# A transformer layer's input projection in an order written by hand, with its filling work dealt anew

## The chip, the core and the metric

The kernel runs on one core of one Trainium2 chip. The metric is device time of one execution in microseconds (us), lower is better. A core has five engines that run side by side, each with its own queue of instructions in a fixed order: TensorE (PE, matrix products), VectorE (DVE), ScalarE (ACT), GpSimd (POOL) and SyncE (SP, which here only issues DMA transfers). Products land in PSUM, which DVE and ACT read; everything else lives in SBUF.

## The reference, cut to what matters

One decoder layer on 1024 tokens of width 1024, in float32:

```
xn   = rmsnorm(h, pre_mix_norm)
proj = xn @ w_in                       # queries, keys, gates of retention, latents cq, ckv, kr
ret  = silu(rg) * groupnorm(retention(rope(rq), rope(rk), rv))
mla  = softmax(causal(q @ k^T)) @ v    # 8 heads; q, k, v from rmsnorm(cq), rmsnorm(ckv), rope(kr)
mix  = concat([ret, mla]) @ w_o
h    = h + rmsnorm(mix, post_mix_norm)
hn   = rmsnorm(h, pre_ffn_norm)
h    = h + rmsnorm((silu(hn @ w_gate) * (hn @ w_up)) @ w_down, post_ffn_norm)
h    = h + rmsnorm(p @ w_ple_proj, ple_norm) * sigmoid(h @ w_ple_gate + b)
```

## The kernel before, in words

Every matrix product is made of three: each operand is split into a high part (an ACT cast, L81) and the rest (a DVE subtraction, L82), and high x high, low x high and high x low are summed in PSUM. The sequence is cut into 8 row tiles of 128 tokens.

**Input projection of the latents** (`pa`, to 82 us). For each tile: x is loaded (`xt`), ACT squares it with a row sum (L186), DVE and POOL make the factor (`rsqrt`: L111 on DVE, a power on POOL L113), DVE multiplies (L188, with the norm weights `wpre`, which a DMA has copied to all partitions), PE turns eight blocks of 128x128 (`ptf`, L175), ACT and DVE split the result into `bh` and `bl`, and PE does 48 products of 336 columns (`pa`, L94). The weights come in six transfers `raw_a`, each split into `hi_a` and `lo_a`. ACT and DVE then norm the result (L241 to L250). The rotary tables (some 20 small DVE instructions from L258 on and two Sin on ACT, after the load of the positions `posi`) are written behind the loop. A scheduler in the build chooses each engine's order from the program and its own cost figures, so work of different tiles and tables lies mixed.

**Attention** (375 to 563 us). Eight heads, two column groups each; a group ends with `os` (L648) and its store to `mo`. Between the groups PE gets pieces of filling work: for the first heads preparations, and from head 2 on pieces of the output projection's retention part (`fill` into `od`, 16 pieces of 12 products with 512 columns), dealt by the line `advance(gen, "fo"[gg], ...)` in the head loop.

**Output projection and norms** (563 to 680 us, `project(n)` and `operands(n)`). For each tile n, `mo` is loaded, split (`mh` by ACT, `ml` by POOL; two buffers each), PE does 24 products `po` into a PSUM tile pair (two buffers), DVE adds `od` (L715), ACT squares with a row sum (L717; the squares themselves are of no use and go to the PSUM tile), then factor, scale and add (L719, L720), a second Square (L723, again into the PSUM tile), scale (L725, L726). `operands(n)` turns the result with PE (`ptx`); for tiles 4 to 7 POOL first makes sums and differences of tile pairs (L739 to L742). After it come the first gate and up products (`gu`), whose weights are loaded to `graw` and `duo[0]` and summed by POOL (`weight_sums`, L793 to L796). From 680 us to about 1080 us `gu` runs, then the down projection, then the last gate.

Of the kernel before, what the change touches and what calls it, by code (L numbers as in the profile page):

```python
# [62 lines left out]
def hybrid_layer(ctx: ExitStack, tc: tile.TileContext, a: dict, out: bass.AP):  # L63
# [105 lines left out]
    def to_features(src, t, tags, bh, bl):  # L169
        ts = slice(t * P, (t + 1) * P)  # L170
        for c in range(2):
            pt = ps1("ptf", tags[c])
            for i in range(4):
                k = 4 * c + i
                pe.transpose(pt[:, i * P : (i + 1) * P], src[:, k * P : (k + 1) * P], ident)  # L175
            v = pt.rearrange("p (k n) -> p k n", k=4)
            split(bh[c][:, :, ts], bl[c][:, :, ts], v)

# [5 lines left out]
    def norm_in(t, xt):  # L184
        ss = small.tile([P, 1], F32, name="ss")
        act.activation(cq[:, t, :512].bitcast(BF16), xt, AF.Square, accum_out=ss)  # L186
        rsqrt(ss, ss, 1.0 / D)
        dve.scalar_tensor_tensor(out=xt, in0=xt, scalar=ss, in1=wpre, op0=ALU.mult, op1=ALU.mult)  # L188
        to_features(xt, t, "tt", bh, bl)
# [7 lines left out]
    for i in range(0, 16, AB):
        m = min(AB, 16 - i)
        stage = tabs.tile([P, S], F32, tag=["tcos", "tsin"][i // AB - 4], name=f"raw_a{i}") if i // AB >= 4 else None
        wa.append(slot(a["w_a"][i : i + m].rearrange("b p n -> p b n"), AC * m, name=f"a{i}", stage=stage))  # L200
        if i // AB == 3:
            xt = load_in(1)
# [4 lines left out]


# [15 lines left out]
    for t in range(NT):  # L224
        if t:
            norm_in(t, xt)
            if t + 1 < NT:
                xt = load_in(t + 1)
        pt = ps2(f"pa{t}")
        ca, cb = pt[:, 0:AC], pt[:, 512 : 512 + AC]  # L230
        for c, dst in ((0, ca), (1, cb)):
            products(
                dst,
                [
                    (*bx(k, slice(t * P, (t + 1) * P)), wa_of(0, k, c), wa_of(1, k, c))
                    for k in range(8)
                ],
            )
        sst = small.tile([P, 3], F32, name="sst")
        dst = cq[:, t, :]  # L240
        act.activation(dst[:, :AC], ca, AF.Square, scale=_f32(QL**-0.5), accum_out=sst[:, 0:1])  # L241
        act.activation(dst[:, AC:QL], cb[:, : QL - AC], AF.Square, scale=_f32(QL**-0.5), accum_out=sst[:, 2:3])
        act.activation(dst[:, QL : QL + KVL], cb[:, QL - AC : QL - AC + KVL], AF.Square, scale=_f32(KVL**-0.5),
                       accum_out=sst[:, 1:2])
        dve.tensor_tensor(out=sst[:, 0:1], in0=sst[:, 0:1], in1=sst[:, 2:3], op=ALU.add)
        fac = small.tile([P, 2], F32, name="fac")
        rsqrt(fac, sst[:, 0:2], 1.0)
        dve.tensor_scalar(out=dst[:, :AC], in0=ca, scalar1=fac[:, 0:1], scalar2=None, op0=ALU.mult)
        dve.tensor_scalar(out=dst[:, AC:QL], in0=cb[:, : QL - AC], scalar1=fac[:, 0:1], scalar2=None, op0=ALU.mult)
        dve.tensor_scalar(out=dst[:, QL : QL + KVL], in0=cb[:, QL - AC : QL - AC + KVL], scalar1=fac[:, 1:2],  # L250
                          scalar2=None, op0=ALU.mult)
        act.copy(out=krt[:, t, :], in_=cb[:, QL - AC + KVL : AC])

    RA, HR = RD // 2, ROPE // 2
    posi = tb.tile([P, NT], I32, name="posi")
    sp.dma_start(out=posi, in_=a["pos"])
    posf = tb.tile([P, NT], F32, name="posf")
    dve.tensor_copy(out=posf, in_=posi)  # L258
    angm, sin, cos = [tb.tile([P, NT, HR], F32, name=n) for n in ("angm", "msin", "mcos")]
    dve.tensor_tensor(  # L260
        out=angm,
        in0=posf.unsqueeze(2).broadcast_to([P, NT, HR]),
        in1=inv.unsqueeze(1).broadcast_to([P, NT, HR]),
        op=ALU.mult,
    )
    rotary(angm, sin, cos)
# [2 lines left out]
    dve.tensor_copy(out=mc[:, :, :HR], in_=cos)
    dve.tensor_copy(out=mc[:, :, HR:], in_=cos)  # L270
    dve.tensor_scalar(out=ms[:, :, :HR], in0=sin, scalar1=-1.0, scalar2=None, op0=ALU.mult)
    dve.tensor_copy(out=ms[:, :, HR:], in_=sin)
# [432 lines left out]
    def project(n):  # L705
# [462 lines left out]
```

## Time and profile before

| | |
|---|---|
| median of 3 runs | 1399.54 us (1396.53 to 1400.5) |
| profiled execution | 1400.68 us |
| its span in the trace | 1398.9 us, so 1.8 us lie outside |
| PE busy | 1336.5 us, 96% of the span |
| DVE, ACT, POOL busy | 770.9, 541.8, 461.8 us |

Times in rows are from the span's start. A row of the timeline names its start, its duration, the engine, the line, the operation, the tile written and read, how many alike follow, and in brackets the idle time of that engine ahead of it and what ended it.

### The profile page before, as it was taken

What the parts mean: (1) busy time and instruction counts of PE and PEld (TensorE: products, weight loads), DVE (VectorE), ACT (ScalarE), POOL (GpSimd) and SP (SyncE); (2) the same over time, 40 slices, a digit from 0 to 9 for tenths busy, and PEclk for the clock granted to TensorE, in tenths of its full rate; (3) what the DMA queues carried; (4) which work ended last, traced back from release to release, by engine and by line L of the source; (5) the groups of instructions that cost most, each with busy time, mean ns of one, the idle gap of its engine ahead of it and who ended that gap; (6) DMA issues with size and microseconds to landing.
All of it is one profiled execution on the core that took longest, in us unless ns stands there. A gap on an engine that the chain in (4) does not pass through costs nothing.

```text
span 1398.9 us, 18091 instructions
## 1 busy us (share of the span) xinstructions
PE 1336.5 (96%) x6756; PEld 1134.4 (81%) x6756; DVE 770.9 (55%) x1193; ACT 541.8 (39%) x898; POOL 461.8 (33%) x341
## 2 busy tenths in 40 slices
PE   7999999999989999887999999999999999999997
PEld 6987988988778887665788888888888788888886
DVE  6445637445566676488445444444445554474645
ACT  5443321011565555355343333333334444344521
POOL 1100000000363333248577666666664100012500
PEclk9999999999999999998999999999999999999999
DMA  7127831212474641743344344433346876565422
GB/s 251 46 92 250 265 118 39 75 23 60 143 232 123 200 131 30 273 135 123 121 165 149 146 173 173 169 138 144 140 178 218 269 234 211 178 218 193 138 102 75
DMA packets 85304, 214.73 MB, mean 153 GB/s; under 512 B 8992, under 2 KB 23840, under 8 KB 79584
## 3 DMA queue, kind: packets, MB, share of 16 engines
q1 hardware_dynamic: 85216, 213.58, 45.5%
q8 instruction: 53, 0.87, 0.3%
q14 instruction: 35, 0.29, 0.1%
HBM read 144.86 MB, written 67.63 MB: 152 GB/s over the span
## 4 chain that ended last, share of the span: by engine, by line
PE 83%; DMA 4%; DVE 4%; POOL 3%; issue 3%; ACT 2%; SPq 1%; DVEq 0%; ACTq 0%; POOLq 0%
PE gu L834 29%; PE db L1011 7%; PE pqk L94 6%; PE pg L94 6%; PE da L1011 6%; PE pa L94 4%; PE fill L94 3%; PE prv L94 3%; PE sc L94 3%; PE ptp L630 2%; PE prg L94 2%; PE pge L94 2%; PE po L642 1%; PE pq L94 1%; PE po L641 1%
## 5 line engine op out<-in xcount | busy, mean ns | idle before, releaser
L834 PE MATMUL gu<-x,gh 128*128 128x512 f32 x1232 | 383.6, 393 | 6.3 <-ACT po L723 5.6
L834 PEld LDWEIGHTS gu<-x,gh 128*128 128x128 f32 x1232 | 233.2, 190 | 55.7 <-ACT po L723 5.8
L834 PE MATMUL gu<-x,gl 128*128 128x512 f32 x616 | 241.2, 392 | 0.4 <-DVE gl L82 0.4
L834 PEld LDWEIGHTS gu<-x,gl 128*128 128x128 f32 x616 | 116.7, 189 | 25.1 <-DVE gl L82 0.7
L845 ACT COPY duo<-gu 128x512 f32<-128x512 f32 x66 | 38.9, 589 | 189.3 <-PE gu L834 189.3
L621 POOL TENSOR_TENSOR pr<-pr,ri 128x128 f32<-128x128 f32 (+3 forms) x64 | 74.8, 1178 | 105.7 <-DVE ri L620 98.4
L113 POOL TENSOR_TENSOR s<-s,mhalf 128x1 f32<-128x1 f32 x32 | 23.9, 752 | 238.4 <-DVE s L111 238.3
L113 POOL TENSOR_TENSOR gf<-gf,mhalf 128x4 f32<-128x4 f32 x8 | 8.1, 1008 | 266.7 <-DVE gf L111 266.7
L82 DVE TENSOR_TENSOR gl<-strip,gh 128x1024 fp32r<-128x1024 f32 (+1 forms) x44 | 61.6, 1399 | 33.3 <-ACT gh L81 33.3
L82 DVE TENSOR_TENSOR x<-draw,x 128x1024 fp32r<-128x1024 f32 (+1 forms) x43 | 48.1, 1135 | 46.9 <-ACT x L81 46.9
L82 DVE TENSOR_TENSOR gl<-graw,gh 128x1024 fp32r<-128x1024 f32 x22 | 33.8, 1538 | 72.5 <-ACT gh L81 72.5
L81 ACT CAST x<-draw 128x1024 fp32r<-128x1024 f32 (+1 forms) x47 | 45.2, 979 | 73.0 <-PE db L1011 20.6
L82 DVE TENSOR_TENSOR gl<-duo,gh 128x1024 fp32r<-128x1024 f32 x22 | 29.5, 1343 | 67.9 <-ACT gh L81 67.9
L850 DVE TENSOR_TENSOR duo<-gu,duo 128x512 f32<-128x512 f32 x66 | 45.4, 687 | 38.0 <-PE gu L834 37.9
L82 DVE TENSOR_TENSOR tl<-ptp,th 128x512 fp32r<-128x512 f32 (+1 forms) x80 | 49.8, 633 | 24.7 <-ACT th L81 23.7
L94 PE MATMUL pg<-x,x 128*128 128x512 f32 (+1 forms) x255 | 58.9, 378 | 0.0
L81 ACT CAST th<-ptp 128x512 fp32r<-128x512 f32 (+1 forms) x80 | 42.4, 544 | 41.9 <-PE ptp L630 41.6
L855 POOL TENSOR_TENSOR duo<-duo 128x512 f32<-128x512 f32 x11 | 23.3, 2122 | 103.2 <-DVE duo L818 103.2
L617 ACT ACTIVATE pr<-sc,nm 128x128 f32<-128x128 f32 (+3 forms) x64 | 47.7, 747 | 18.7 <-DVE nm L612 11.1
L94 PEld LDWEIGHTS pg<-x,x 128*128 128x128 f32 x255 | 45.8, 188 | 8.6
L612 DVE CUSTOM_DVE_ANT_0 sc<-sc,cmask 128x128 f32<-128x128 f32 (+3 forms) x64 | 48.0, 770 | 7.7 <-PE sc L94 7.3
L94 PE MATMUL pqk<-bl,hi_r 128*128 128x512 f32 x128 | 50.7, 396 | 0.0
(368 smaller groups left out, 3418.5 us busy)
## 6 DMA issues: line engine op xcount, KB each, us to landing
draw<-ld SPq DMA_DIRECT2D x58, 256.0 KB, 3.8
graw<-in_w_gate SPq DMA_DIRECT2D x11, 1024.0 KB, 8.6
duo<-in_w_up SPq DMA_DIRECT2D x11, 1024.0 KB, 4.7
duo<-in_w_down SPq DMA_DIRECT2D x11, 1024.0 KB, 5.1
td<-duo SPq DMA_DIRECT2D x11, 1024.0 KB, 4.4
ld<-duo SPq DMA_DIRECT2D x11, 1024.0 KB, 4.4
draw<-td SPq DMA_DIRECT2D x36, 256.0 KB, 4.1
ld<-duo SPq DMA_DIRECT2D x11, 768.0 KB, 6.7
```

The costliest lines, as they stand in the source:

```text
L81: act.copy(out=hi, in_=src)
L82: sub.tensor_tensor(out=lo, in0=src, in1=hi.bitcast(F32), op=ALU.subtract)
L94: pe.matmul(dst, l, r, start=(m == 0), stop=(m == n - 1))
L113: pool.tensor_tensor(out=dst, in0=dst, in1=mhalf[:, :n], op=ALU.pow)
L612: dve.tensor_tensor_reduce(out=sv, in0=sv, in1=cmask[:, S - n :].rearrange("p (c n) -> p c n", c=nc_), scale=-1.0, scalar=3.0e38, op0=ALU. ...
L617: act.activation(pr_[:, :n].rearrange("p (c n) -> p c n", c=nc_), sv, AF.Exp, bias=nm, scale=-1.0, accum_out=rs)
L621: pool.tensor_tensor(out=pr_[:, :n], in0=pr_[:, :n], in1=ri.broadcast_to([P, n]), op=ALU.mult)
L630: pe.transpose(pt[:, m * P : (m + 1) * P], pb[qq][:, kk * P : (kk + 1) * P], ident)
L834: pe.matmul(dst, l[:, at, ks], r[:, k, :], start=(n in (0, 1, 3) and x == 0), stop=(x == 11), skip_group_check=True)
L845: act.copy(out=s[nm], in_=dst)
L850: dve.tensor_tensor(out=s[nm], in0=dst, in1=s[nm], op=ALU.add)
L1011: pe.matmul(banks[j], l[:, ls], r[:, rs_], start=(fresh and q == 0 and m == 0), stop=(q == NQ - 1 and m == 2), skip_group_check=True)
```

## The change

Six things are changed.

1. The input projection is written as one function `head()`, whose instructions keep the order in which they stand (`tc.manual_schedule()`). Tiles 0 and 1 are computed side by side, by weight transfer: `part(t, i)` is the nine products of tile t with the weights of transfer i. x of tile 1 is loaded ahead of the weights.
2. The norm weights are loaded as one row of 4 KB, not as a 512 KB copy for all partitions. PE spreads the row with two products against ones (`spread`), and DVE copies the result (L247).
3. PE gets 9 and 12 products on ones without use (`turn`) ahead of and behind the spreading.
4. The rotary tables are one block, after tile 4.
5. `FILL` deals the output projection's pieces otherwise: before, heads 2 to 5 had 3 each, heads 6 and 7 one each, and 2 were left for the end; now heads 2 to 7 have 1, 3, 2, 2, 2 and 3 (the last three inside the last column group of head 7), and 3 are left.
6. The squares of no use in `project` go to a free corner of SBUF (`xt[6]`), so that DVE's add is the PSUM tile's last reader. The first gate weights go to `duo[0]` and the first up weights to the tile `graw`, the other way round than before.

```diff
-    norm_in(0, xt)
...
+    def head():
+        junk = ps1("turn", "f")[:, :P]
+
+        def turn(n):
+            for _ in range(n):
+                pe.matmul(junk, minus, minus, start=True, stop=True)
+
+        sp.dma_start(out=wpre[:1], in_=a["w_pre"])
+        xts = [load_in(0)]
...
+        def half(t, c):
+            pt = ps1("ptf")
+            for i in range(4):
+                k = 4 * c + i
+                pe.transpose(pt[:, i * P : (i + 1) * P], xts[t][:, k * P : (k + 1) * P], ident)
+            ts = slice(t * P, (t + 1) * P)
+            split(bh[c][:, :, ts], bl[c][:, :, ts], pt.rearrange("p (k n) -> p k n", k=4))
+            if c and t + 2 < NT:
+                xts.append(load_in(t + 2))
...
+        pt = ps2("spread")
+        turn(9)
+        for c in range(2):
+            cs = slice(c * 512, (c + 1) * 512)
+            pe.matmul(pt[:, cs], minus[:1], wpre[:1, cs], start=True, stop=True)
+        dve.tensor_copy(out=wpre, in_=pt)
+        turn(12)
+        ss = [squares(0), squares(1)]
+        norm(0, ss[0])
+        weights()
+        half(0, 0)
...
+        for t in range(2, NT):
+            pas[t] = ps2(f"pa{t}")
+            for k in range(8):
+                in_product(t, k, 0)
+            if t + 1 < NT:
+                ready(t + 1)
+            evict(t - 1)
+            if t + 1 < NT:
+                half(t + 1, 0)
+                half(t + 1, 1)
+            for k in range(8):
+                in_product(t, k, 1)
+            if t == 4:
+                tables()
+        evict(NT - 1)
...
+    FILL = (0, 1), (2, 1), (1, 1), (1, 1), (1, 1), (0, 0)
...
+                    if h == NH - 1 and g == 3 and jj < 3:
+                        advance(gen, "o", 1)
...
-                advance(gen, "fo"[gg], (2, 1)[gg] if h < 6 else 1 - gg)
+                advance(gen, "fo"[gg], FILL[h - 2][gg])
...
+        junk = xt[6][:, :, :, 3 * P :].rearrange("p h k n -> p (h k) n")
         ss = small.tile([P, 1], F32, name="s3")
-        act.activation(pt, mix, AF.Square, accum_out=ss)
+        act.activation(junk, mix.rearrange("p (b n) -> p b n", b=8), AF.Square, accum_out=ss)
...
+    sp.dma_start(out=duo[0].rearrange("p (i n) -> p i n", i=4), in_=a["w_gate"][0])
...
-    graw = [pg_.tile([P, 4, HALF], F32, name="graw"), quad[0]]
+    graw = [quad[0], pg_.tile([P, 4, HALF], F32, name="graw")]
```

What this does to the order of instructions is shown at three places. The first is DVE's queue in the input projection, between the split of tile 5 and the factor of tile 6 (`ss`; `angm`, `mc`, `ms` are the tables). After the change:

```order
L323 TENSOR_SCALAR angm<-angm 128x128
L325 SCALAR_TENSOR_TENSOR angm<-angm 128x128
L326 TENSOR_SCALAR angm<-angm 128x128
L346 COPY mc<-mcos 128x8x16
L347 COPY mc<-mcos 128x8x16
L348 TENSOR_SCALAR ms<-msin 128x8x16
L349 COPY ms<-msin 128x8x16
L111 TENSOR_SCALAR ss<-ss 128x1
L236 SCALAR_TENSOR_TENSOR xt<-xt,ss,wpre 128x1024
```

These are the last seven of 20 table instructions in a row, and tile 6's factor and scaling stand behind them. Before the change the tables lay between the work of tiles 1 to 3:

```order
L217 SCALAR_TENSOR_TENSOR angm<-mcos,angm 128x128
L217 SCALAR_TENSOR_TENSOR angm<-msin,angm 128x128
L111 TENSOR_SCALAR ss<-ss 128x1
L217 SCALAR_TENSOR_TENSOR angm<-mcos,angm 128x128
L248 TENSOR_SCALAR cq<-pa_235,fac 128x336
L249 TENSOR_SCALAR cq<-pa_235,fac 128x48
```

So the tables have moved from early and scattered to late and in one piece.

The second place is ACT's queue at the start of the output projection (`mh` are the splits for the tiles in order, the ACTIVATE rows are the Squares and scalings of the norms). Before:

```order
L81 CAST mh_5759<-strip_5743 128x512
L81 CAST mh_5805<-strip_5743 128x512
L717 ACTIVATE po3_5763,s3_5789<-duo3_5741 128x1024
L81 CAST mh_5851<-duo2_5740 128x512
L723 ACTIVATE po3_5763,s3_5796<-duo4_5742 128x1024
L717 ACTIVATE po3_5809,s3_5835<-duo0_5738 128x1024
```

After the change:

```order
L81 CAST mh_5790<-strip_5774 128x512
L81 CAST mh_5836<-strip_5774 128x512
L81 CAST mh_5882<-duo2_5771 128x512
L81 CAST mh_5941<-duo2_5771 128x512
L81 CAST mh_6000<-strip_5774 128x512
L803 ACTIVATE x6_5765,s3_5820<-duo3_5772 128x8x128
L81 CAST mh_6058<-strip_5774 128x512
L809 ACTIVATE x6_5765,s3_5827<-duo4_5773 128x8x128
```

Tile 0's first Square now stands behind five splits, where it stood behind two.

The third place is POOL's queue ahead of the first operand sums (L739 before and L825 after are the first sum of tile 4; L793 and L880 the first of a weight block; L113 the power of a norm's factor). After:

```order
L113 TENSOR_TENSOR s_6030<-s_6030,mhalf 128x1
L880 TENSOR_TENSOR strip<-graw 128x512
L883 TENSOR_TENSOR graw<-graw 128x512
L113 TENSOR_TENSOR s_6037<-s_6037,mhalf 128x1
L113 TENSOR_TENSOR s_6088<-s_6088,mhalf 128x1
L825 TENSOR_TENSOR duo_5772<-duo_5769,duo_5772 128x512
```

Before, all eight weight sums stood between the operand sums of tiles 6 and 7:

```order
L742 TENSOR_TENSOR duo_5740<-duo_5740,duo_5742 128x512
L793 TENSOR_TENSOR strip<-duo_5738 128x512
L113 TENSOR_TENSOR s_6199<-s_6199,mhalf 128x1
L796 TENSOR_TENSOR duo_5738<-duo_5738 128x512
L793 TENSOR_TENSOR strip<-graw 128x512
```

Two of the eight have moved ahead of tile 4's operands; the other six stay where they were.

## Rows read from the trace of the kernel before

**Rows 1.** The page's first part: span, and busy time of PE.

```profile
span 1398.9 us, 18091 instructions
...
PE 1336.5 (96%) x6756; PEld 1134.4 (81%) x6756; DVE 770.9 (55%) x1193; ACT 541.8 (39%) x898; POOL 461.8 (33%) x341
```

**Rows 2.** Windows: length, then busy (count) of each engine, granted clock, DMA share, GB/s.

```profile
426.36:550.00 123.64, 118.36 (x743) 105.48 (x741) 87.22 (x204) 68.65 (x151) 49.62 (x42) 1.00 0.46 132
550.00:562.90 12.90, 10.40 (x46) 8.34 (x46) 4.81 (x9) 6.28 (x12) 1.89 (x1) 0.74 0.05 11
550.00:675.00 125.00, 97.57 (x418) 76.89 (x419) 80.89 (x92) 56.51 (x92) 62.39 (x49) 0.87 0.44 155
```

**Rows 3.** PE's waits: for what, us in total, times, longest.

```profile
PE po L94 <- ACT po L723: 9.2, 6, 3.6
...
PE gu L834 <- ACT po L723: 5.6, 1, 5.6
```

**Rows 4.** Timeline of the input projection, engines mixed.

```profile
9.49 1.21 DVE L82 TENSOR_TENSOR lo_a<-raw_a,hi_a 128x1008 fp32r<-128x1008 f32 x1 [1.73 <-ACT hi_a L81]
...
24.39 0.28 DVE L217 SCALAR_TENSOR_TENSOR angm<-msin,angm 128x128 f32<-128x128 f32 x1
...
32.54 0.42 PE L94 MATMUL pa<-hi_a,bh 128*128 128x336 f32 x1 [1.05 <-ACT bh L81]
...
58.03 0.33 SPq L181 DMA_DIRECT2D xt<-in_x  x1
...
61.66 1.06 ACT L186 ACTIVATE cq<-xt 128x1024 bf16<-128x1024 f32 x1 [0.75 <-DMA xt<-in_x]
...
62.84 0.15 DVE L111 TENSOR_SCALAR ss<-ss 128x1 f32<-128x1 f32 x1 [1.21 <-ACT cq L186]
63.72 1.28 DVE L188 SCALAR_TENSOR_TENSOR xt<-xt,ss,wpre 128x1024 f32<-128x1024 f32 x1 [0.72 <-POOL ss L113]
```

**Rows 5.** Timeline of attention from head 1's last `os` to the filling behind it.

```profile
426.36 0.68 DVE L648 TENSOR_TENSOR os<-po,os 64x512 f32<-64x512 f32 x1
...
548.63 0.95 PE L630 MATMUL ptp<-pack,pr 128*128 128x128 f32 x7
...
554.84 1.72 PE L630 MATMUL ptp<-pack,pr 128*128 128x128 f32 x7
...
562.93 0.69 DVE L648 TENSOR_TENSOR os<-po,os 64x512 f32<-64x512 f32 x1 [1.26 <-ACT os L647]
```

**Rows 6.** Timeline of the output projection's start, ACT, DVE and PE.

```profile
571.91 0.39 PE L94 MATMUL po<-bh,mh 128*128 128x512 f32 x1
572.13 0.39 PE L94 MATMUL po<-bl,mh 128*128 128x512 f32 x1
...
579.32 1.03 ACT L717 ACTIVATE po<-duo 128x1024 f32<-128x1024 f32 x1 [7.80 <-DVE duo L715]
...
581.32 1.28 DVE L719 SCALAR_TENSOR_TENSOR duo<-duo,s,strip 128x1024 f32<-128x1024 f32 x1 [0.67 <-POOL s L113]
```

**Rows 7.** Timeline of POOL's sums, and of PE at the first products of tile 4 to 7.

```profile
623.02 1.29 POOL L739 TENSOR_TENSOR duo<-duo,duo 128x512 f32<-128x512 f32 x1
...
649.46 1.30 POOL L793 TENSOR_TENSOR strip<-duo 128x512 f32<-128x512 f32 x1 [0.64 <-DMA duo<-in_w_up]
...
664.26 1.29 POOL L795 TENSOR_TENSOR strip<-duo,strip 128x512 f32<-128x512 f32 x1
...
670.61 1.27 POOL L742 TENSOR_TENSOR duo<-duo,duo 128x512 f32<-128x512 f32 x1
...
671.25 1.52 PE L834 MATMUL gu<-x,gh 128*128 128x512 f32 x2 [0.68 <-ACT x L81]
...
679.39 1.47 PE L686 MATMUL ptx<-pack,duo 128*128 128x128 f32 x12
```

**Rows 8.** Groups of instructions by line: the Squares into PSUM, and into SBUF.

```profile
L723 ACT ACTIVATE po<-duo 128x1024 f32<-128x1024 f32 x8 | 8.2, 1026 | 14.3 <-DVE duo L720 14.3
...
L186 ACT ACTIVATE cq<-xt 128x1024 bf16<-128x1024 f32 x8 | 8.5, 1058 | 7.5 <-DMA xt<-in_x 7.5
```

More of the change, by code (lines that the diff above doesn't have):

```diff
@@ L123, in hybrid_layer @@
     mhalf = const.tile([P, 32], F32, name="mhalf")
+    minus = const.tile([P, P], F32, name="minus")
+    pool.memset(minus, 1.0)
     pool.memset(mhalf, -0.5)
@@ L168, in hybrid_layer @@
     cq = pa.tile([P, NT, AW], F32, name="cq")
[L169 to L177, printed above, removed]
     def load_in(t):
@@ L182, in load_in @@
         return xt
[L184 to L189, printed above, removed]
     krt = tb.tile([P, NT, ROPE], F32, name="krt")
-    xt = load_in(0)
-    sp.dma_start(out=wpre, in_=a["w_pre"].broadcast_to([P, D]))
-    sp.dma_start(out=pack, in_=a["pack"])
-    norm_in(0, xt)
     wa = []
[L197 to L202, printed above, removed]
     def wa_of(n, k, c):
@@ L206, in wa_of, with in_product, weights, ready @@
         return wa[i // AB][n][:, (i % AB) * AC : (i % AB + 1) * AC]
+    def in_product(t, k, c):
+        xh, xl = bx(k, slice(t * P, (t + 1) * P))
+        wh, wl = wa_of(0, k, c), wa_of(1, k, c)
+        for m, (l, r) in enumerate(((xh, wh), (xh, wl), (xl, wh))):
+            pe.matmul(pas[t][:, c * 512 : c * 512 + AC], l, r, start=(k == 0 and m == 0), stop=(k == 7 and m == 2))
+    def head():
[5 more added lines that the diff above has]
+        xts = [load_in(0)]
+        sp.dma_start(out=pack, in_=a["pack"])
+        xts.append(load_in(1))
+        raw_a = []
+        for i in range(0, 16, AB):
+            m = min(AB, 16 - i)
+            raw = tabs.tile([P, S], F32, tag=["tcos", "tsin"][i // AB - 4], name=f"raw_a{i}") if i // AB >= 4 else (
+                raws.tile([P, S], F32, tag="raw", name=f"raw_a{i}"))
+            raw = raw[:, : AC * m]
+            sp.dma_start(out=raw.rearrange("p (b n) -> p b n", b=m), in_=a["w_a"][i : i + m].rearrange("b p n -> p b n"))
+            raw_a.append(raw)
+        def weights():
+            i = len(wa)
+            wa.append([t[:, : raw_a[i].shape[1]] for t in pair(f"a{i}")])
+            split(*wa[i], raw_a[i])
+        def ready(t):
+            norm(t, squares(t))
+        def half(t, c):
[7 more added lines that the diff above has]
+                xts.append(load_in(t + 2))
+        def squares(t):
+            s = small.tile([P, 1], F32, name="ss")
+            act.activation(cq[:, t, :512].bitcast(BF16), xts[t], AF.Square, accum_out=s)
+            return s
+        def norm(t, s):
+            rsqrt(s, s, 1.0 / D)
+            dve.scalar_tensor_tensor(out=xts[t], in0=xts[t], scalar=s, in1=wpre, op0=ALU.mult, op1=ALU.mult)
+        def part(t, i):
+            for kc in range(i * AB, min(i * AB + AB, 16)):
+                in_product(t, kc // 2, kc % 2)
+        pt = ps2("spread")
[9 more added lines that the diff above has]
+        half(0, 0)
+        for t in range(2):
+            pas[t] = ps2(f"pa{t}")
+        part(0, 0)
+        norm(1, ss[1])
+        weights()
+        half(0, 1)
+        part(0, 1)
+        half(1, 0)
+        part(1, 0)
+        weights()
+        part(0, 2)
+        half(1, 1)
+        part(1, 1)
+        for i in range(3, 6):
+            weights()
+            part(0, i)
+            if i == 3:
+                part(1, 2)
+        ready(2)
+        evict(0)
+        part(1, 3)
+        half(2, 0)
+        half(2, 1)
+        part(1, 4)
+        part(1, 5)
+        for t in range(2, NT):
+            pas[t] = ps2(f"pa{t}")
+            for k in range(8):
[11 more added lines that the diff above has]
+        evict(NT - 1)
@@ new lines, in evict @@
+    def evict(t):
+        pt = pas[t]
+        ca, cb = pt[:, 0:AC], pt[:, 512 : 512 + AC]
+        sst = small.tile([P, 3], F32, name="sst")
+        dst = cq[:, t, :]
+        act.activation(dst[:, :AC], ca, AF.Square, scale=_f32(QL**-0.5), accum_out=sst[:, 0:1])
+        act.activation(dst[:, AC:QL], cb[:, : QL - AC], AF.Square, scale=_f32(QL**-0.5), accum_out=sst[:, 2:3])
+        act.activation(dst[:, QL : QL + KVL], cb[:, QL - AC : QL - AC + KVL], AF.Square, scale=_f32(KVL**-0.5),
+                       accum_out=sst[:, 1:2])
+        dve.tensor_tensor(out=sst[:, 0:1], in0=sst[:, 0:1], in1=sst[:, 2:3], op=ALU.add)
+        fac = small.tile([P, 2], F32, name="fac")
+        rsqrt(fac, sst[:, 0:2], 1.0)
+        dve.tensor_scalar(out=dst[:, :AC], in0=ca, scalar1=fac[:, 0:1], scalar2=None, op0=ALU.mult)
+        dve.tensor_scalar(out=dst[:, AC:QL], in0=cb[:, : QL - AC], scalar1=fac[:, 0:1], scalar2=None, op0=ALU.mult)
+        dve.tensor_scalar(out=dst[:, QL : QL + KVL], in0=cb[:, QL - AC : QL - AC + KVL], scalar1=fac[:, 1:2],
+                          scalar2=None, op0=ALU.mult)
+        act.copy(out=krt[:, t, :], in_=cb[:, QL - AC + KVL : AC])
@@ L209, in rotary @@
+    pas = {}
     def rotary(ang, kh, kl):
@@ L222, in rotary @@
         act.activation(kl, ang, AF.Sin)
[L224 to L252, printed above, removed]
@@ L254, in hybrid_layer @@
-    RA, HR = RD // 2, ROPE // 2
[L255 to L266, printed above, removed]
+    RA, HR = RD // 2, ROPE // 2
@@ L267, in hybrid_layer, with tables @@
     mc = tb.tile([P, NT, ROPE], F32, name="mc")
     ms = tb.tile([P, NT, ROPE], F32, name="ms")
[L269 to L272, printed above, removed]
+    def tables():
+        posi = tb.tile([P, NT], I32, name="posi")
+        sp.dma_start(out=posi, in_=a["pos"])
+        posf = tb.tile([P, NT], F32, name="posf")
+        dve.tensor_copy(out=posf, in_=posi)
+        angm, sin, cos = [tb.tile([P, NT, HR], F32, name=n) for n in ("angm", "msin", "mcos")]
+        dve.tensor_tensor(
+            out=angm,
+            in0=posf.unsqueeze(2).broadcast_to([P, NT, HR]),
+            in1=inv.unsqueeze(1).broadcast_to([P, NT, HR]),
+            op=ALU.mult,
+        )
+        rotary(angm, sin, cos)
+        dve.tensor_copy(out=mc[:, :, :HR], in_=cos)
+        dve.tensor_copy(out=mc[:, :, HR:], in_=cos)
+        dve.tensor_scalar(out=ms[:, :, :HR], in0=sin, scalar1=-1.0, scalar2=None, op0=ALU.mult)
+        dve.tensor_copy(out=ms[:, :, HR:], in_=sin)
@@ L275, in hybrid_layer @@
+    with tc.manual_schedule():
+        head()
     kr = tb.tile([P, NT, ROPE], F32, name="kr")
@@ L887, in when @@
         todo[i].append((f, args))
-    load(0)
     load(1)
```

2 lines of the change are left out of this document (1 added, 1 removed).

## Prediction

> **What bounds the kernel now.** I read the page's busy times first: PE works 1336.5 of 1398.9 us [rows 1], so a gain must come from the 62 us in which it idles, or from stretches at the lower of its two clock levels (1.2 GHz, not 2.4). The windows say where these lie. From 550 to 675 us PE works 97.57 of 125 us, 27.4 idle, at a mean granted clock of 0.87; from head 1's end to 550 it works 118.36 of 123.64, 5.3 idle; in attention's last 12.9 us it is busy 10.40 at 0.74 [rows 2]. Nearly everything else is PE-bound. PE's waits name the releasers: `po` waited 9.2 us and `gu` 5.6 for the Squares that go to PSUM [rows 3]. DVE is busy 80.89 of the 125 us and POOL 62.39 [rows 2], so behind those waits stands a chain of norms that needs ACT, DVE and POOL in turn. Removing a wait on PSUM helps only as far as this chain comes earlier too.
>
> The profiled execution took 1400.68 us, 1.8 outside its span and 1.1 above the median of 1399.54. I sum against 1400.68 and take off 1.1 at the end.
>
> **Input projection, tiles side by side.** Before, the first split of weights runs on DVE at 9.49 and tile 2's first product starts at 32.54, after 1.05 of waiting [rows 4]. Afterwards the first product is still bound by x, the spread weights and `lo_a`. I walk DVE's queue: copy of `spread` (1.2), tile 0's scaling (1.28) to about 9.5, then six `lo_a` of 1.21 (the last a third), and four splits and tile 1's scaling between them [rows 4]. Tile 0's products then need transfer 3's weights at 22, and the last of both tiles end, with tile 2 turned as well, near 31: 1.5 us earlier than 32.54. The 4 KB row instead of 512 KB saves a transfer's place in the queue, but x of tile 1 takes that place. The bounds: 3 earlier if the splits never hold PE, and 3 later if the 23 added products run at the low level, end behind x, and hold tile 0's turning (seven turnings of 128 columns take 1.72 us at the low level and 0.95 at the full one [rows 5]; if a product on ones is worth two of them, the 21 take some 10 us instead of 6, beside the spreading: an estimate). I take -1.5.
>
> The clock here is told by the rows: attention's seven turnings take 0.95 us at 548.63 and 1.72 at 554.84, after PE had stood still several times [rows 5], so an idle PE falls to the lower level. The Trainium skill ("TensorE: Matmul & The Clock Gate", section "What's actually happening") says that the throttled state is the default and activity releases it. By that rule the products on ones would give the first products the full level; whether DVE's splits let PE use it is the walk above.
>
> **Input projection, tables.** Twenty table instructions on DVE, 0.28 or a little less each [rows 4], are some 4.5 us, and hid between other work before. Now they stand in one piece ahead of tile 6's factor, and wait for the positions, whose load is queued behind the last x. Such an x was issued at 58.03 and the Square that waits for it ran at 61.66, 3.6 later [rows 4]. From the middle of tile 4, where the last x is now issued (about 54), the block starts at 55.5 to 58, and with the two Sin and ACT's Square behind them tile 6's factor is 5 to 8 us later; the chain factor, power, scaling takes 62.84 to 65.0 [rows 4]. PE wants the turned tile at about 61, and gets it at 63.4 to 66: it stands 2 to 5 us, since the second half of tile 5 is queued behind those turnings. I take 3.5, between both ends. If tile 5's own work covered it, it would cost nothing. The input projection together: +2.0, from -3 to +8.
>
> **Attention with the pieces dealt anew.** A piece is 12 products 0.22 apart [rows 6], 2.7 us. Heads 2 to 7 had 14, now 13: -2.7. Head 7 now has three at its end. There PE idled 2.5 of 12.9 us [rows 2], and the row of turnings at 1.72 against 0.95 [rows 5] shows about 6 us at half speed, 3 us lost; both can be filled: -5.4. The dealing among heads 2, 4, 5 and 6 is neutral as long as PE paces them, which 118.36 of 123.64 says. So `os` of head 7, at 562.93, comes 8.1 earlier. Bounds: -2.7, if other engines pace the heads with few pieces, and -12, if most of the 5.3 goes too.
>
> **Output projection.** With the Squares off PSUM, PE runs tiles 0 to 5 in one go. But ACT's order puts five `mh` ahead of tile 0's first Square, and the fifth needs a buffer that the third tile's products free. On the basis of the old end of attention: `po` starts at 571.91 [rows 6], 12 `po`, 12 of the left-over piece and 60 `po` take 19.1, `mh` 0.6, the Square with its sum 1.2, the power and waits 0.9, so the first scaling (L719) is at 593.9 instead of 581.32 [rows 6], 12.6 later. Behind it on ACT are every later norm and operand; who waits is DVE, then POOL.
>
> Then the norms catch up, since three adds and most splits are done by then. The next fixed point is POOL's first sum for tile 4, at 623.02 [rows 7]. Two weight sums now stand ahead of it, whose load waits for the last `po`: 156 products from 571.91 reach 607, with the last two tiles and the turnings between them 620, the load some 7, the sums 3.5, so 630.5 to 635.4 with the waits for norms. From 623.02 to the end of tile 7's sums at 671.9 are 48.9; the eight weight sums in it (649.46 to 665.55 [rows 7]) are six now, 4 to 8 us less. Tile 4 to 7's first products, at 671.25 [rows 7], thus come 7.5 to 12.4 later less 4 to 8: -0.5 to +8.3, and I take +5.0 near the upper middle, because the late start of the norms shows in each of these numbers.
>
> The 24 products behind (671.25 to 679.39, 8.1 us) ran partly at the low level; at 0.23 each they take 5.5. If PE no longer stands still just ahead of them, -2.6.
>
> Sixteen Squares now write SBUF. The row with PSUM as target has 1026 ns, the one with SBUF 1058 [rows 8]: 0.03 each, 0.5 us on an engine that is not full. The swap of `graw` and `duo[0]` turns places round and I find no queue that it delays later: 0. The Trainium skill ("ScalarE: Activation LUTs", section "Step-by-step: what each stage is for") says that ACT writes PSUM faster than SBUF, which speaks against this edit; it states no price, and by the two rows the sum stays.
>
> **Sum.** 2.0 - 8.1 + 5.0 - 2.6 = -3.7: 1397.0 against the profiled execution, 1396 against the median.
>
> **Rivals.**
> *The norms catch up wholly* (and the tables are covered): -8.1 - 2.6 = -10.7, 1389. For it: PSUM waits of 14.8 us vanish [rows 3], and DVE has 44 us free in the 125. Against: ACT's order.
> *Slower: the late first norm isn't caught up.* 12.6 late less 8.1, with PE standing ahead of the operands as now, so at the low level again, and 2.0: +6.5, 1406. It decides from a catch-up under some 2 us of the 12.6, or under 5 if the clock is not regained. For it: DVE worked at 65% and POOL at 50% of that stretch [rows 2], each waiting on the other.
> *The pieces don't pace attention*: only -2.7 there, and 1401, no change.
>
> **How the numbers follow.** A measurement tells about 0.3% (4.2 us) from no change, so faster is below 1395.3, slower above 1403.7. Chances: the sum as it stands 0.47, with its own range 1391 to 1402 (0.20 of it faster, 0.25 same, 0.02 slower); full catch-up 0.22, faster; no catch-up 0.19, slower; attention not paced 0.12 (0.08 same, 0.04 slower). Together faster 0.42, same 0.33, slower 0.25. I predict 1396; the range 1385 to 1408 reaches from beyond full catch-up to beyond none.
>
> **What would show it.** Right: attention's last `os` near 555; a gap of 2 to 5 us on PE ahead of tile 6's turning, with DVE on table work; the first scaling 3 to 5 us later than 581.32; POOL's first sum of tile 4 behind two weight sums; the products behind the last operands at the full level. Wrong: the last `os` at 560 or beyond; no gap at tile 6; PE's idle time from 550 to 675 hardly under 27 us, or under 15; a transfer of the gate or up weights that ends the wait ahead of `gu`.

## The result, and the profile after

The changed kernel takes 1413.84 us (median of 4 runs, 1412.82 to 1419.22) against 1399.38 of the kernel before beside it: 1.0119 times, interval 1.0095 to 1.0143. It is slower by 14 us, and outside the predicted range. I read the page first, then windows of the stretches of [rows 2].

```profile
span 1411.7 us, 18196 instructions
...
PE 1346.3 (95%) x6802; PEld 1141.2 (81%) x6802; DVE 770.5 (55%) x1194; ACT 541.7 (38%) x898; POOL 462.2 (33%) x342
```

Windows of after: length, then busy time (count) of PE, PE's loads, DVE, ACT and POOL, granted clock, DMA share, GB/s.

```profile
550.00:675.00 125.00, 96.35 (x453) 77.70 (x452) 80.02 (x98) 55.27 (x92) 54.21 (x44) 0.85 0.44 159
571.00:625.00 54.00, 50.61 (x227) 41.11 (x228) 25.08 (x27) 15.38 (x25) 13.75 (x13) 1.00 0.60 225
625.00:675.00 50.00, 26.29 (x108) 19.82 (x108) 42.66 (x48) 29.09 (x48) 34.80 (x27) 0.62 0.41 139
```

PE's busy time grew by 9.8 us [rows 1]; the products on ones and the spreading alone take 13.3 (below). From 550 to 675, in which attention now ends 8 us later, it idles 28.65 us, where 27.4 stood before [rows 2]: the waits for PSUM are gone, and PE works 50.61 of 54 us behind attention, but then only 26.29 of 50 at a granted clock of 0.62. The idle time has moved behind the output projection's products. PE's waits (for what, us in total, times, longest) say for whom:

```profile
PE ptx L771 <- ACT duo L812: 12.8, 2, 8.7
PE ptx L771 <- POOL duo L825: 6.8, 4, 2.5
PE ptf L223 <- DVE sst L303: 4.9, 1, 4.9
...
PE pa L187 <- DVE lo_a L82: 2.0, 2, 1.2
```

The 14.8 us that PE waited for Squares into PSUM [rows 3] are replaced by 12.8 us in two waits for `duo`, that is for late norms (`ptx` turns the normed tiles), and 4.9 at tile 6 of the input projection. Cut at marks that both programs have (the end of the input projection is the start of PE's next row), the spans compare thus:

| stretch | before | after | difference |
|---|---|---|---|
| start to tile 2's first product | 32.54 | 37.59 | +5.05 |
| to the last product of the input projection | 49.66 | 55.85 | +6.2 |
| to head 1's last `os` | 344.16 | 345.47 | +1.3 |
| to head 7's last `os` | 136.57 | 131.98 | -4.6 |
| to the first products of tile 4 to 7 | 108.32 | 115.69 | +7.4 |
| to the end | 727.65 | 725.12 | -2.5 |
| span | 1398.9 | 1411.7 | +12.8 |

The timeline of after at the two places where it lost, engines mixed. First the input projection:

```profile
0.99 4.21 PE L196 MATMUL turn<-minus 128*128 128x128 f32 x18 [0.99 <-POOL mhalf L126]
5.13 3.78 PE L246 MATMUL spread<-wpre,minus 1*128 1x512 f32 x4
8.84 5.33 PE L196 MATMUL turn<-minus 128*128 128x128 f32 x24
14.01 0.60 PE L223 MATMUL ptf<-pack,xt 128*128 128x128 f32 x4
15.28 0.42 PE L187 MATMUL pa<-hi_a,bh 128*128 128x336 f32 x1 [0.68 <-ACT bh L81]
...
19.14 0.42 PE L187 MATMUL pa<-lo_a,bh 128*128 128x336 f32 x1 [1.19 <-DVE lo_a L82]
...
20.48 0.60 PE L223 MATMUL ptf<-pack,xt 128*128 128x128 f32 x4
...
21.74 0.69 DVE L82 TENSOR_TENSOR bl<-ptf,bh 128x512 fp32r<-128x512 f32 x1 [2.05 <-ACT bh L81]
22.67 1.21 DVE L82 TENSOR_TENSOR lo_a<-raw_a,hi_a 128x1008 fp32r<-128x1008 f32 x1 [0.24 <-ACT hi_a L81]
26.53 0.69 DVE L82 TENSOR_TENSOR bl<-ptf,bh 128x512 fp32r<-128x512 f32 x1 [2.65 <-ACT bh L81]
...
51.11 8.59 SPq L173 DMA_DIRECT2D xt<-in_x  x2
59.75 0.42 SPq L335 DMA_DIRECT2D posi<-in_pos  x1
63.02 0.17 DVE L337 CAST posf<-posi 128x8 f32<-128x8 int32 x1 [2.17 <-DMA posi<-in_pos]
...
68.69 0.22 DVE L349 COPY ms<-msin 128x128 f32<-128x128 f32 x1
70.20 1.29 DVE L236 SCALAR_TENSOR_TENSOR xt<-xt,ss,wpre 128x1024 f32<-128x1024 f32 x1 [0.73 <-POOL ss L113]
71.63 1.69 PE L223 MATMUL ptf<-pack,xt 128*128 128x128 f32 x8 [4.92 <-DVE sst L303]
```

Three things are to be seen. The first turning comes at 14.01 instead of 7.81, behind the products on ones. DVE stands idle 2.05 and 2.65 us ahead of two splits of x (`bl`), while splits of weights (`lo_a`) stand behind them in its queue. And the tables, from 63.02 to 68.9, wait 2.17 us for positions loaded behind the last x, and hold tile 6's scaling; PE idles 4.92 us, and the turning behind it takes 1.69 for 8, where 1.03 is the time at the full level (E7 below).

Then the output projection:

```profile
594.48 0.62 ACT L81 CAST mh<-duo 128x512 fp32r<-128x512 f32 x1 [3.09 <-PE po L94]
599.92 0.62 ACT L81 CAST mh<-strip 128x512 fp32r<-128x512 f32 x1 [4.82 <-PE po L94]
600.45 1.06 ACT L803 ACTIVATE x<-duo 128x1024 fp32r<-128x1024 f32 x1
...
589.28 1.23 DVE L800 TENSOR_TENSOR duo<-po,duo 128x1024 f32<-128x1024 f32 x1 [2.08 <-PE po L94]
594.66 1.23 DVE L800 TENSOR_TENSOR duo<-po,duo 128x1024 f32<-128x1024 f32 x1 [4.16 <-PE po L94]
600.16 1.23 DVE L800 TENSOR_TENSOR duo<-po,duo 128x1024 f32<-128x1024 f32 x1 [4.27 <-PE po L94]
602.47 1.28 DVE L805 SCALAR_TENSOR_TENSOR duo<-duo,s,strip 128x1024 f32<-128x1024 f32 x1 [0.69 <-POOL s L113]
...
634.81 1.49 POOL L880 TENSOR_TENSOR strip<-graw 128x512 f32<-128x512 f32 x1 [0.96 <-PE ptx L771]
636.38 2.13 POOL L883 TENSOR_TENSOR graw<-graw 128x512 f32<-128x512 f32 x1
643.87 1.70 POOL L825 TENSOR_TENSOR duo<-duo,duo 128x512 f32<-128x512 f32 x1 [0.74 <-ACT duo L812]
643.85 1.11 PE L771 MATMUL ptx<-pack,duo 128*128 128x128 f32 x4 [8.69 <-ACT duo L812]
686.58 1.52 PE L921 MATMUL gu<-x,gh 128*128 128x512 f32 x2 [0.68 <-ACT x L81]
```

Tile 0's sum is ready at 590.5 (the first L800), but its Square starts at 600.45, behind an `mh` that waits for the third tile's products. DVE stands between three adds with 4.2 us idle ahead of the second and third, so that the first scaling is at 602.47.

Times of these marks after head 7's last `os` (562.93 in the kernel before, 570.89 here) are called E+ below. The first scaling is at E+18.4 before and E+31.6 after; the products of tile 4 to 7 at E+108.3 and E+115.7.

### The profile page after: what moved, and what is told of

It is laid out like the page before. It is cut to its first block, busy times and chain, and to the rows that moved or that the text cites. A ratio compares the mean times of both kernels' runs of the same rounds, so it can differ in the third digit from the quotient of the medians.

```text
span 1411.7 us, 18196 instructions
## 1 busy us (share of the span) xinstructions
PE 1346.3 (95%) x6802; PEld 1141.2 (81%) x6802; DVE 770.5 (55%) x1194; ACT 541.7 (38%) x898; POOL 462.2 (33%) x342
## 4 chain that ended last, share of the span: by engine, by line
PE 85%; POOL 3%; DVE 3%; issue 3%; DMA 2%; ACT 2%; SPq 1%; ACTq 0%; DVEq 0%; POOLq 0%
PE gu L921 29%; PE db L1097 8%; PE pqk L94 6%; PE pg L94 6%; PE da L1097 6%; PE pa L187 3%; PE prv L94 3%; PE po L94 3%; PE sc L94 3%; PE fill L94 3%; PE pge L94 2%; PE prg L94 2%; PE ptp L713 2%; PE pq L94 1%; PE po L727 1%
## 5 line engine op out<-in xcount | busy, mean ns | idle before, releaser
L113 POOL TENSOR_TENSOR s<-s,mhalf 128x1 f32<-128x1 f32 x32 | 24.9, 783 | 239.5 <-DVE s L111 239.5
L113 POOL TENSOR_TENSOR gf<-gf,mhalf 128x4 f32<-128x4 f32 x8 | 8.1, 1008 | 267.8 <-DVE gf L111 267.8
L82 DVE TENSOR_TENSOR gl<-duo,gh 128x1024 fp32r<-128x1024 f32 x22 | 33.1, 1503 | 71.4 <-ACT gh L81 71.4
L82 DVE TENSOR_TENSOR tl<-ptp,th 128x512 fp32r<-128x512 f32 (+1 forms) x80 | 49.6, 633 | 16.4 <-ACT th L81 15.1
L700 ACT ACTIVATE pr<-sc,nm 128x128 f32<-128x128 f32 (+3 forms) x64 | 47.7, 746 | 18.4 <-PE ptp L713 6.5
```

What stands on the lines that cost most here:

```text
L82: sub.tensor_tensor(out=lo, in0=src, in1=hi.bitcast(F32), op=ALU.subtract)
L113: pool.tensor_tensor(out=dst, in0=dst, in1=mhalf[:, :n], op=ALU.pow)
L700: act.activation(pr_[:, :n].rearrange("p (c n) -> p c n", c=nc_), sv, AF.Exp, bias=nm, scale=-1.0, accum_out=rs)
```

## Experiments

The theory at the outset: the head (the input projection's new start) and the late first norm both lose, and the pieces gain. The rival: one of the two loses alone, and the rest follows from it. Each experiment's ratio is to the kernel before on the same chip.

**E1 to E4: the parts apart.** E1 is the changed kernel with the head of before, E2 the head alone, E3 the dealing of pieces alone, E4 the Squares alone, each in the kernel before.

```diff
 E1: -    with tc.manual_schedule():
     -        head()                       (before's loop and tables instead)
...
 E3: +    FILL = (0, 1), (2, 1), (1, 1), (1, 1), (1, 1), (0, 0)
...
     +                    if h == NH - 1 and g == 3 and jj < 3:
     +                        advance(gen, "o", 1)
...
     +                advance(gen, "fo"[gg], FILL[h - 2][gg])
...
 E4: -        act.activation(pt, mix, AF.Square, accum_out=ss)
     +        act.activation(junk, mix.rearrange("p (b n) -> p b n", b=8), AF.Square, accum_out=ss)
...                                        (the second Square of a tile likewise)
```

> The kernel before with everything of the change but the input projection's new order (pieces dealt anew, squares to SBUF, graw and duo[0] swapped). Theory A, the loss lies in the input projection: by the marks in the two traces it is 11.1 us of the 14, so this one takes 1400 to 1403 us: attention 4.6 shorter, the output projection 7.4 longer, the products behind it 2.5 shorter. Theory B, the late norms of the output projection come from the head's other end (other prefetches, other buffers): then this one is at 1393 to 1396.

> The kernel before with the input projection's new order alone. Theory A: the first product of tile 2 about 5.5 later, the tables' block 5.6 more, so 1410 to 1413. Theory B, part of the delay is hidden behind what follows: 1403 to 1406.

> The kernel before with the pieces dealt anew alone; ACT's order at the output projection keeps two splits ahead of the first Square. Theory A, the dealing itself gains about 4.6 and nothing takes it back: 1394 to 1396. Theory B, one piece more behind attention costs what was gained ahead of it: 1398 to 1400.

> The kernel before with the squares written to SBUF alone; ACT's order then has three splits ahead of the first Square, not two and not five. Theory A, PE's waits on PSUM were worth little, since the norms behind them set the end: 1397 to 1401. Theory B, they were worth their 14.8 us of waiting, half of it at least: 1388 to 1393.

Measured, with 1398.25 for the kernel before: E1 1403.48 (1.0059, 1.0040 to 1.0078), E2 1402.38 (1.0033, 1.0014 to 1.0052), E3 1391.81 (0.9959, 0.9943 to 0.9975), E4 1398.88 (1.0010, 0.9994 to 1.0026). The pieces alone gain 6.4 us, the Squares alone do nothing, the head alone loses 4. The parts don't add up: E1, which holds pieces, Squares and swap, is 12 us above the pieces alone. Its first scaling is at E+30.6, that of E3 at E+20.8 and of E4 at E+22.4. In E3 the Square (L721) writes PSUM still:

```profile
556.94 0.68 DVE L652 TENSOR_TENSOR os<-po,os 64x512 f32<-64x512 f32 x1 [1.26 <-ACT os L651]
...
576.92 0.15 DVE L111 TENSOR_SCALAR s<-s 128x1 f32<-128x1 f32 x1 [1.22 <-ACT po L721]
577.74 2.30 DVE L723 SCALAR_TENSOR_TENSOR duo<-duo,s,strip 128x1024 f32<-128x1024 f32 x1 [0.67 <-POOL s L113]
```

In E2 the products of the input projection end at 91.29, 9.1 later than before (82.20), but the stretch from E to tile 4's products was 102.4 instead of 108.3: with the first scaling at E+18.4 as before, POOL's first sum for tile 4 came at E+54.9 instead of E+60.1. So a part's time alone isn't its share in the whole, and the forecast of 1410 to 1413 for E2, which added up the delays, missed. What made that stretch shorter was not tested.

**E5 to E8: what holds the late norm, and what the head loses.** E5 is E3 with the Squares; E6 is E1 with ACT's order mended; E7 is the changed kernel with the tables in five portions and their positions loaded right behind the weights, E8 the changed kernel without products on ones.

```diff
 E6: +        if n >= 3:
     +            with tc.issue_after(squared[n - 3]):   (the Square of tile n - 3)
     +                split(mh, ml, mt, sub=pool)
 E7: -            if t == 4:
     -                tables()
...
     +        steps = tables()               (ahead of the loads of the weights)
...
     +        next(steps)                    (behind them: the load of the positions)
...
     +            next(steps, None)          (a portion behind each of tiles 2 to 6)
...
 E8: -        turn(9)
     +        turn(0)
     -        turn(12)
     +        turn(0)
```

> The kernel before with the pieces dealt anew and the squares to SBUF, without the swap of graw and duo[0]. ACT's order has the five splits ahead of the first Square again, POOL's order has no weight sum ahead of tile 4's operands. Theory A, the five splits cost what is lost: some 1400 to 1404, like the run without the head. Theory B, the up weights that POOL and ACT wait for (the swap) cost it: 1391 to 1394, like the pieces alone.

> The kernel of e1 (everything but the head), with one thing more: the split of tile n (from tile 3 on) is issued on ACT behind the first Square of tile n-3. Two words of order, no work more or less; three splits then stand ahead of the first Square, not five. Theory A: the first scaling comes 19 to 23 us behind attention's last os, not 31, and the time falls from 1403.5 to 1390 to 1396. Theory B (the swap and its weights): the products of tile 4 to 7 stay late, 1400 to 1404.

> The changed kernel with the tables in five portions after tiles 2 to 6 and the positions loaded behind the weights. Theory A, the one block cost 4.9 us of idle PE and some of the clock: the end of the input projection falls from 93.4 to 87 to 88.5, the time from 1413.8 to 1407 to 1409. Theory B, the gap is made up for later anyway: 1412 to 1415.

> The changed kernel without the 21 products on ones. Theory A, they hold up the spreading ahead of them and tile 0's turning behind them: the first product comes at 10 to 12, not 15.3, tile 2's first at 34 to 36, not 37.6, and the time is 1410 to 1412. Theory B, they give back more by the clock than they take: the input projection ends later than 93.4, and the time is 1414 to 1417.

Measured, with 1397.33 for before: E5 1404.84 (1.0060, 1.0039 to 1.0082), E6 1402.68 (1.0047, 1.0031 to 1.0064), E7 1407.72 (1.0082, 1.0056 to 1.0107), E8 1414.44 (1.0119, 1.0102 to 1.0137).

E5 has no swap of `graw` and `duo[0]` and is as slow as E1: the swap isn't the cause, pieces and Squares together are. E6 put the Square on time and gained nothing that counts, since DVE's queue held the scaling as well. The timeline of E6, ACT and DVE:

```profile
577.70 1.06 ACT L728 ACTIVATE x<-duo 128x1024 fp32r<-128x1024 f32 x1
...
585.26 1.22 DVE L725 TENSOR_TENSOR duo<-po,duo 128x1024 f32<-128x1024 f32 x1 [4.27 <-DMA od<-fill]
...
587.21 2.27 DVE L731 SCALAR_TENSOR_TENSOR duo<-duo,s,strip 128x1024 f32<-128x1024 f32 x1 [0.67 <-POOL s L113]
```

The Square ends at 578.9 and its sum is read, but tile 0's factor waits behind the add of tile 2 at 585.26. So my theory of ACT's order was half of it.

In E7 the stretch from tile 2's first product to the last one takes 49.6 us, as before (49.66), instead of 55.85. PE's row at tile 6 has no wait:

```profile
63.53 1.03 PE L225 MATMUL ptf<-pack,xt 128*128 128x128 f32 x8
```

The late block of tables, with its positions, thus cost 6.3 us of PE's time, and the kernel gains 5 by the ratios when it is spread. E7 takes away both the one piece and the wait for the positions; what each is worth alone was not tested. E7's tile 2 starts at 34.55, not at 37.59, though PE, DVE and ACT have the same instructions up to there; the last section comes back to this. E8 was a miss by both theories: without the products on ones tile 2's first product comes at 33.94, 3.65 earlier than in the changed kernel, and the time is no lower (1.0119 both). So they gain nothing here, and what is won at this mark does not arrive at the end.

**E9 to E12: both orders mended.** E9 adds the same edge for DVE to E6 (the add of tile n behind the second add of tile n - 2). E11 is E5 with both edges, one tile tighter on DVE; E12 is E7 with those of E11. E10 is E3 with the tiles side by side, tables in portions, but the broadcast load and no products on ones; x of tile 1 is loaded behind the second transfer of weights, no longer ahead of the first, and its scaling stands behind the next splits.

```diff
 E9:  +        if n >= 2:
      +            with tc.issue_after(added[n - 2]):      (E11, E12: n - 1)
      +                dve.tensor_tensor(out=mix, in0=pt, in1=mix, op=ALU.add)
...
 E10: -        pt = ps2("spread")
      -        turn(9)
...
      -            pe.matmul(pt[:, cs], minus[:1], wpre[:1, cs], start=True, stop=True)
      -        dve.tensor_copy(out=wpre, in_=pt)
      -        turn(12)
...
      +        sp.dma_start(out=wpre, in_=a["w_pre"].broadcast_to([P, D]))
...
      +            if len(raw_a) == 2:
      +                xts.append(load_in(1))
...
```

> The kernel of e6 with one more word of order: DVE's add of tile n (from tile 2 on) is issued behind the second add (L720 before the change) of tile n-2. In e6 the first Square was on time (577.7, 20.6 us behind attention's last os), but DVE had the adds of tiles 0, 1 and 2 ahead of tile 0's factor, and the third waits for the third tile's products (585.3), so the first scaling stayed 30 us behind. Theory A, two queues hold the same wait and either is enough: now the first scaling comes 21 to 23 us behind os, tile 4's first sum 58 to 62 behind it, and the time is 1388 to 1394. Theory B, the squares to SBUF cost by something else (POOL and DVE slow each other): 1400 to 1404 still.

> The pieces dealt anew, and the changed input projection in another form: tiles 0 and 1 side by side, but the norm weights copied to all partitions by the transfer as before (no spreading and no products on ones), x of tile 1 loaded behind the second weight transfer, the tables in five portions. Squares and swap as in the kernel before. Theory A, the lost time lay in the spreading, the products on ones and the tables, and the tiles side by side gain 1 to 2 us: tile 2's first product at 30 to 32, the input projection ends at 80 to 82, the time is 1389 to 1392. Theory B, tiles side by side lose by themselves, through DVE's order: tile 2 at 33 to 35, 1393 to 1396.

> The kernel of e5 (pieces dealt anew, squares to SBUF, no swap) with both words of order, DVE's tighter than in e9: the split of tile n behind the first Square of tile n-3, DVE's add of tile n behind the second add of tile n-1. Theory A: the first scaling 20 to 22 us behind the last os (30.7 in e5, 24.8 in e9, 20.8 with the pieces alone), and 1390 to 1394, 11 to 14 less than e5 and like the pieces alone: the squares in SBUF give nothing once the order is good. Rival: with the order mended they gain by themselves, 1383 to 1389.

> The whole changed kernel with the tables in five portions (as e7) and both words of order (as e11). If the losses are three separate ones, they add up: 1413.8 less 6 for the tables less 9 for the order, 1397 to 1400, with tile 2's first product still at 34 to 37 (tiles side by side not mended). Rival: the parts are not additive, since the scheduler deals the later order anew: 1403 or more, or below 1395.

Measured: E9 1394.57 (0.9978, 0.9961 to 0.9994) and E10 1400.02 (1.0013, 0.9995 to 1.0031) with 1397.65 for before; E11 1393.47 (0.9965, 0.9950 to 0.9980) and E12 1393.53 (0.9969, 0.9955 to 0.9983) with 1398.47. By the ratios E9 is 11 us below E1, and E11 13 below E5. The first scaling goes from E+30.7 (E5) to E+22.4 (E11), where DVE's timeline has one add ahead of it and not three:

```profile
575.23 1.22 DVE L729 TENSOR_TENSOR duo<-po,duo 128x1024 f32<-128x1024 f32 x1 [2.08 <-PE po L94]
579.13 0.15 DVE L111 TENSOR_SCALAR s<-s 128x1 f32<-128x1 f32 x1 [2.68 <-ACT x L732]
579.97 1.29 DVE L735 SCALAR_TENSOR_TENSOR duo<-duo,s,strip 128x1024 f32<-128x1024 f32 x1 [0.68 <-POOL s L113]
```

That the order on the two queues is what the Squares cost is therefore shown (an edge on DVE alone was not run). With it mended they gain nothing measurable over the pieces alone (0.9965 and 0.9959). E12 keeps every part of the change but the place of the tables and the order behind attention, and takes some 20 us off it, 4 to 6 more than the separate gains added up to in its forecast. E10 was a miss: without spreading, side by side came out later, not earlier, with tile 2's first product at 37.74. Its real products start at 9.91, as before, but PE then stands 2.24 us for tile 1's scaling, up to 18.41, and the granted clock from 18.4 to 27 is 0.60.

**E13 and E14: which part of the start loses.** E12 with the tiles in turn again, with spreading (E13) and without (E14: the start of the kernel before, in the hand-made order; pieces, Squares, swap, both edges and the tables in portions stay). E13 loads x of tile 1 ahead of the weights, as the changed kernel does, E14 behind the fourth transfer of weights, as the kernel before does.

```diff
 E13: -        part(0, 0)
      -        norm(1, ss[1])
      +        weights()
      +        half(0, 1)
      +        part(0, 0)                    (all of tile 0, then tile 1)
...
 E14: -        pt = ps2("spread")            (as in E10: broadcast load, no turn)
...
      +            if len(raw_a) == 4:
      +                xts.append(load_in(1))
...
```

> The kernel of e12, with the first two tiles one after the other again (all of tile 0's products, then tile 1's), and the norm weights still spread by PE with the products on ones ahead of them. Tile 2's first product was at 34.67 in e12, at 32.54 in the kernel before. Theory A (the side by side order, with its splits of x between the splits of weights, is at fault, the spreading is not): tile 2's first product at 32.5 to 33.5, and 1391.5 to 1392.5, 1 to 2 below e12. Theory B (the spreading is at fault: the first product of the projection, which waits for the copy of the spread weights, stays at 14 to 15 us instead of 10): tile 2's first product at 35 or later, and 1393.5 or more.

> As e13, and the norm weights come by the broadcast load again, with no products on ones: the head of the kernel before, written into the hand-made order. Theory A: like e13, tile 2's first product at 32.5 to 33.5 and the same time within 1 us. Theory B: tile 2's first product at 32.5, 2 or more ahead of e13, and the time 2 or more below it. If both parts cost something: between, with e13 1 to 2 us slower than this one.

Measured, with 1397.07 for before: E13 1393.68 (0.9973, 0.9959 to 0.9988), E14 1386.66 (0.9927, 0.9906 to 0.9948). E14 is the best kernel of this study, 10 us below the kernel before. Tile 2's first product, the table of two by two:

| | side by side | in turn |
|---|---|---|
| spread by PE | 34.67 (E12) | 31.77 (E13) |
| broadcast load | 37.74 (E10) | 29.65 (E14) |

With spreading, side by side costs 2.9 us by an experiment that changes the order alone. The other differences are not as clean: 8.1 with the broadcast load, 2.1 for spreading in turn and 3.1 saved by it side by side each hold the place of tile 1's x as well, and E10 lost at tile 1's scaling. So both theories hold a part; that the two edits interact is not shown. PE's and DVE's timeline of E13 shows where spreading loses:

```profile
4.69 1.98 PE L248 MATMUL spread<-wpre,minus 1*128 1x512 f32 x4
6.60 4.58 PE L196 MATMUL turn<-minus 128*128 128x128 f32 x24
11.01 1.04 PE L225 MATMUL ptf<-pack,xt 128*128 128x128 f32 x8
...
6.71 1.23 DVE L249 COPY wpre<-spread 128x1024 f32<-128x1024 f32 x1 [6.71 <-PE spread L248]
8.73 1.28 DVE L238 SCALAR_TENSOR_TENSOR xt<-xt,ss,wpre 128x1024 f32<-128x1024 f32 x1 [0.74 <-POOL ss L113]
```

In E14 the same scaling starts at 6.48 and the turning at 7.82:

```profile
6.48 1.28 DVE L239 SCALAR_TENSOR_TENSOR xt<-xt,ss,wpre 128x1024 f32<-128x1024 f32 x1 [0.89 <-DMA wpre<-in_w_pre]
...
7.82 1.97 PE L226 MATMUL ptf<-pack,xt 128*128 128x128 f32 x8 [7.82 <-DVE xt L239]
```

The scaling comes 2.25 us later for the copy, and the second batch of products on ones keeps PE until 11.0, one us beyond the scaling's end. The price in time, with the place of tile 1's x in it, was larger than at this mark: E13 is 7 us above E14, with 2.1 at this mark, 4.9 at the last `os` and 5.7 at tile 4's products. Where it grows was not followed.

## Why the prediction was wrong

Of the 16.5 us between the sum (-3.7) and the span (+12.8), the input projection made 9.2, attention 3.5, the output projection 2.4 and the stretch up to head 1's end, which the sum left out, 1.3. These are shares of one profiled execution; E2 and E8 show that a gain or loss at one mark need not arrive whole at the end.

**Tiles side by side** (-1.5, at most 3 later): +5.05, wrong in sign. The step that failed walked DVE's queue as if DVE paced it. The queue is in a fixed order with ACT's, and a split of x waits for a turning that stands on PE behind products, which wait for splits of weights in their turn: the turning at 20.48 comes behind nine products of tile 0, one of which had waited 1.19 us for `lo_a`, and the rows above show 2.05 and 2.65 us of idle DVE with splits of weights queued behind. E12 and E13 show that side by side loses 2.9 with spreading; E10 and E14, which differ in the place of tile 1's x too, point the same way with the broadcast load. The products on ones took 9.5 us, near the estimate of 10, but with the spreading they hold the first turning until 14.0, and the bound of 3 didn't hold that. This part of the miss is not the order's: E2 has the same instructions up to tile 2, and there, as in E7 and E12, the first turning comes at 10.9 to 11.0 and tile 2's first product at 34.55 to 34.95, 2.0 to 2.4 later than before and within the bound. The other 2.6 to 3.0 of the 5.05 are the low level at which the profiled execution of the changed kernel ran its start; why it did stays open.

**Tables** (+3.5, from 2 to 5): the mechanism was right, down to PE's gap of 4.92 ahead of tile 6's turning. E7 measures the term at 6.3, beyond its bound of 5. I left out that the level falls in the gap: the granted clock of after from 72 to 80 is 0.79, with tile 6's turning at 1.69.

**Attention** (-8.1): -4.6 here, -4.9 in E3. Mis-sized: if the piece less is worth its 2.7, filling the end brought some 2 more, not 5.4. From [rows 2, 5] it was seen that the end was slow, not that all of that slowness could be filled.

**Output projection.** The first scaling came as the sum had it: 12.6 later predicted, 13.2 measured against E. The net at tile 4's products was +7.4 where I took +5.0 and bounded it by +8.3: inside, mis-sized by 2.4. But this term was a matter of order, and I saw only half of its cause. I named five `mh` on ACT; DVE's three adds held the scaling just as long (E6), so that the number was met in part by luck, and it came free with both edges (E9, E11). **Clock** (-2.6): the total came (-2.5), but by luck, since it was not gained there. The products named are still slow (1.52 us for the first two, as in [rows 7]), their 24 take 7.2 us instead of 8.1, and from 1000 to 1100 PE works 100.00 us where 97.92 stood before. Why that stall is gone was not tested.

**Squares to SBUF** (0): right alone (E4). The row with SBUF as target has 1060 ns, near the 1058 of [rows 8]. What I missed is that the freed PSUM changes the scheduler's order, and most in company with the pieces: the first scaling was at E+22.4 with the Squares alone (E4), at E+30.7 with both (E5). **Swap** (0): right (E1 against E5).

**Rivals.** "The late first norm isn't caught up" described this half of the kernel well: 5.8 us of 13.2 were caught up, near its point of decision, at the low level. Its 1406 lacked the input projection's other 9 us. The full catch-up didn't take place, and the rival with -2.7 alone gave too little by E3. Of the signs named beforehand, the gap at tile 6 and the two weight sums ahead of tile 4's operands came true; the last `os` at 570.89 and 28.65 us of idle PE from 550 to 675 were signs of being wrong.

## What to carry to other kernels

An edit that frees a buffer lets the scheduler run an engine ahead: look at every queue on which the chain's next link stands, not only at the first on which it is late, and pin the order on each (two edges gave 11 to 13 us here). A block of small instructions that was free between other work is paid for when it stands in one piece, behind a late load, ahead of a chain that PE waits for, and then once more in PE's clock. Time parts alone and together: E3 and E4 gave -6.4 and +0.6, both together (E5) +7.5.

## What the runs showed of the hardware

The level of TensorE's clock at the start is not the same in all runs of the same instructions. The spreading took 3.78 us in the changed kernel and 1.98 in E2, E12 and E13, each behind 18 products on ones from 0.99 without a pause; E2's instructions up to there are those of the changed kernel. The granted clock of after from 0 to 9 us nevertheless stands at 1.00, and that of E12 at 0.84 from 5 to 9. At the start it is durations that tell the level, not the column. The window of after:

```profile
5.00:9.00 4.00, 4.00 (x6) 1.33 (x5) 0.06 (x1) 2.35 (x5) 0.00 (x0) 1.00 1.01 359
```

and in E12:

```profile
5.00:9.00 4.00, 4.00 (x19) 2.75 (x19) 1.47 (x3) 2.10 (x4) 0.56 (x1) 0.84 0.98 329
```

The Trainium skill ("TensorE: Matmul & The Clock Gate", section "What's actually happening") says that activity releases the throttled state; here PE was busy from 0.99 on, and the full level came by 4.7 us in one program and not by 8.8 in another. What decides between them no run here shows. E14, without any products on ones, starts its real products at 9.87 at the low level and is 2.1 us ahead of E13 at tile 2; its x of tile 1 is loaded later, too.
